# A transformer block's last output tile: its last unit multiplied in two halves of 256 columns, the final norm's weight and factor in one operation, three output transfers

## The chip, the cores and the metric

One core of a Trainium2 chip runs the whole program. The metric is the device time of one execution in microseconds: the median of three runs before the change is 460.51 us (459.75 to 461.1). The profiled execution took 460.2 us; its first and last instruction lie 458.5 us apart (the span), and 1.7 us lie around them. All times below are microseconds from the span's start unless a length is meant.

## The reference

The input is 256 tokens of width 1024 in float32. One layer: a norm, a projection, three kinds of attention (8 heads of 64 each), gates, an output projection, and then the part that matters here:

```
h   = rmsnorm(x, norm_mlp)
hid = square(relu(h @ w_up))          # [256, 4096]
x   = x + hid @ w_down                # [256, 1024]
out = rmsnorm(x, norm_final)          # x * rsqrt(mean(x*x) + 1e-6) * norm_final
```

The final norm needs the sum of squares over all 1024 columns of a token before any column of its output can be written.

## The kernel before

Every matrix product is made of three: each float32 operand is split into a high part and a remainder (`whi` and `wlo` of the weights, `u_hi` and `u_lo` of the activations), and high x high, low x high and high x low are added up in PSUM. Weights come from memory on the SP queue (`raw`, 1 MB each), ScalarE makes the high part and VectorE the remainder.

The last product is `token_major("d", 32, ...)` at line 752: 32 units of 128 rows of `w_down`. There are four output tiles of 128 tokens by 512 columns, called (t, e): t is the half of the tokens, e the half of the columns. With `by_half` the two tiles of one e stand in one PSUM tensor `ptok` of two banks, one bank each. The first 28 units are done for all four tiles in turn; the last 4 (`tail`) are done tile by tile in the order (0,0), (0,1), (1,0), (1,1), 12 matmuls of 512 columns each (4 units x 3 terms), and after each tile `ready`, here `finish`, is called, so that its work lies beside the next tile's matmuls. After (1,1) nothing is left for TensorE.

`finish` (lines 734 to 750) does this for a tile:

- VectorE adds the product, scaled by `var[t]`, to the residual `x1` (line 736; from PSUM).
- ScalarE squares and sums the first half of the tile's columns (line 232), VectorE the second half (line 233), and VectorE adds the two to what is known so far (line 241, `total`).
- For e = 0, GpSimd multiplies the tile by the norm's weight `g_fin` into `xg` (line 739).
- For e = 1, GpSimd raises `total` to the power -0.5 (line 246, `rstd`), VectorE multiplies the tile by `g_fin` meanwhile (line 743), and then ScalarE scales 384 columns of `xg` by `rstd` (line 747) and VectorE 640 (line 749); each part goes out by its own transfer (line 750), ScalarE's on the ACT queue and VectorE's on the SP queue.

Each engine runs its instructions in the order in which they stand; what another engine makes is waited for at a semaphore, and the waits are put in by the framework from the tiles that an instruction reads and writes.

Of the kernel before, what the change touches and what calls it, by code (L numbers as in the profile page):

```python
# [8 lines left out]
F32 = mybir.dt.float32  # L9
F32R = mybir.dt.float32r  # L10
AF = mybir.ActivationFunctionType
ALU = mybir.AluOpType
PSUM = bass.MemoryType.PSUM

P = 128
S = 256
NT = S // P
D = 1024
# [6 lines left out]
EPS = 1e-6  # L25
# [12 lines left out]
def hybrid_attention_block(ctx, tc, x, norm_mix, w_in, b_forget, w_branch, w_out,  # L38
# [4 lines left out]
    nc = tc.nc  # L43
# [19 lines left out]
    small = ctx.enter_context(tc.tile_pool(name="small", bufs=4))  # L63
# [8 lines left out]
    out = out[0]  # L72
# [27 lines left out]
    ready = {}  # L100
    state = {"next": 0, "used": 0}
# [27 lines left out]
    def weights(which, br, j, i):  # L129
        return ready[which, br, j, i]  # L130

    def used(n=1):

        state["used"] += n
        pump()

    def follow(later, earlier):

        tc.add_manual_dep(later.ins, earlier.ins.name, mybir.DependencyInfo(
            mybir.DependencyClass.NoSync, mybir.DependencyReason.DATA), reason="order on one engine")  # L140
# [7 lines left out]
    def terms(o, pairs, first, last, **kw):  # L148

        for i, (l, r) in enumerate(pairs):  # L150
            nc.tensor.matmul(o, l, r, start=first and i == 0, stop=last and i == len(pairs) - 1, **kw)  # L151
# [77 lines left out]
    def square_sum(src, junk, ss):  # L229

        n = src.shape[-1] // 2
        nc.scalar.activation(junk[:, 0:n], src[:, 0:n], AF.Square, accum_out=ss[:, 0:1])
        nc.vector.tensor_tensor_reduce(junk[:, n:], src[:, n:], src[:, n:], 1.0, 0.0, ALU.mult, ALU.add, ss[:, 1:2])

    def total_square(src, junk, so_far=D * EPS):


        ss = small.tile([P, 2], F32, name="ss", tag="ss")
        square_sum(src, junk, ss)
        total = small.tile([P, 1], F32, name="total", tag="total")  # L240
        made = nc.vector.scalar_tensor_tensor(total, ss[:, 0:1], so_far, ss[:, 1:2], op0=ALU.add, op1=ALU.add)
        return total, made

    def rsqrt(ms):
        rstd = small.tile([P, 1], F32, name="rstd", tag="rstd")
        nc.gpsimd.tensor_tensor(rstd, ms, minus_half, op=ALU.pow)
        return rstd
# [392 lines left out]
    def token_major(which, n_units, hi, lo, tail, order, by_half, ready):  # L640

        pair = [ps.tile([P, 2, 512], F32, name="ptok", tag="s2", bufs=2) for i in range(2)]
        tiles = {(t, e): pair[e][:, t] if by_half else pair[t][:, e] for t in range(NT) for e in range(2)}

        def part(u, t, e, which_terms=(0, 1, 2)):
            c = slice(t * P, (t + 1) * P)
            d = slice(e * 512, (e + 1) * 512)
            wh, wl = weights(which, 0, u // 2, u % 2)
            pairs = [(hi[:, u, c], wh[:, 0, d]), (lo[:, u, c], wh[:, 0, d]), (hi[:, u, c], wl[:, 0, d])]
            terms(tiles[t, e], [pairs[i] for i in which_terms], u == 0 and 0 in which_terms,  # L650
                  u == n_units - 1 and 2 in which_terms)

        for u in range(n_units - tail):
            for some in ((0, 1), (2,)):
                for t in range(NT):
                    for e in range(2):
                        part(u, t, e, some)
            used()
        for t, e in order:
            for u in range(n_units - tail, n_units):  # L660
                part(u, t, e)
            ready(t, e, tiles[t, e])
        used(tail)


    x1 = late.tile([P, NT, D], F32, name="x1")
    for t in range(NT):
        nc.sync.dma_start(x1[:, t], x[t * P:(t + 1) * P])
    g_fin = late.tile([P, D], F32, name="g_fin")
# [16 lines left out]
    def transpose_in(t, e):  # L686
# [4 lines left out]
        if t == 1:  # L691
            for i in range(2):
                split_gain(pts[i], 4 * e + 2 * i, g_mlp, h2[:, :, 0], h2[:, :, 1])

    token_major("o", 8, m_hi, m_lo, 4, [(0, 0), (1, 0), (0, 1), (1, 1)], False, mixed_in)

    mlp = ctx.enter_context(tc.tile_pool(name="mlp", bufs=1))
# [24 lines left out]
    var = []  # L722
    ys = late.tile([P, NT, D], F32, name="ys", tag="m_hi")
# [6 lines left out]
    xg = late.tile([P, D], F32, name="xg", tag="m_lo")  # L730
    sums = {}
    nc.gpsimd.tensor_scalar(g_fin, g_fin, ROOT_D, 0.0, op0=ALU.mult, op1=ALU.add)

    def finish(t, e, p_):
        d = slice(e * 512, (e + 1) * 512)
        nc.vector.scalar_tensor_tensor(x1[:, t, d], p_, var[t], x1[:, t, d], op0=ALU.mult, op1=ALU.add)
        sums[t], made = total_square(x1[:, t, d], ys[:, t, d], sums.get(t, D * EPS))
        if e == 0:
            nc.gpsimd.tensor_tensor(xg[:, d], x1[:, t, d], g_fin[:, d], op=ALU.mult)  # L739
        if e == 0:  # L740
            return
        rstd = rsqrt(sums[t])
        done = nc.vector.tensor_tensor(xg[:, d], x1[:, t, d], g_fin[:, d], op=ALU.mult)
        follow(done, made)
        for i, c in enumerate((slice(0, 384), slice(384, D))):
            if i == 0:
                nc.scalar.activation(ys[:, t, c], xg[:, c], AF.Copy, scale=rstd)  # L747
            else:
                nc.vector.tensor_scalar(ys[:, t, c], xg[:, c], rstd, None, op0=ALU.mult)
            (nc.scalar, nc.sync)[i].dma_start(out[t * P:(t + 1) * P, c], ys[:, t, c])  # L750

    token_major("d", 32, u_hi, u_lo, 4, [(0, 0), (0, 1), (1, 0), (1, 1)], True, finish)


# [26 lines left out]
```

## Time and profile before

| | us |
|---|---|
| median of three runs | 460.51 |
| profiled execution | 460.2 |
| its span | 458.5 |
| TensorE matmul busy | 446.5 (97%) |
| VectorE busy | 326.0 (71%) |
| ScalarE busy | 273.6 (60%) |
| GpSimd busy | 38.5 (8%) |

The page gives busy time, the span in 40 slices, the chain of work that ended last, and the costliest groups of instructions. For a change at the program's very end the single instructions of the last 8 us in order of time say more than the sums: which starts when, how long it takes, and what it had waited for. A row of that view gives the start, the length, the engine (PE is TensorE's matmul, PEld its weight load, DVE VectorE, ACT ScalarE, POOL GpSimd; a q behind the name is the engine's queue, which issues transfers), the line, the operation, output<-inputs, the shape, and in brackets the idle time before it and who ended it.

### The profile page before, as it was taken

The numbers are of one execution on the slowest core, as the hardware profiler recorded it, in microseconds if no ns is written. First come the engines' busy times: TensorE is split into PE (matmuls) and PEld (weight loads), VectorE is DVE, ScalarE is ACT, GpSimd is POOL, SyncE is SP. The second block draws the span as 40 slices with busy tenths as digits, with TensorE's granted clock in tenths as the row PEclk, the third lists the DMA queues.
The fourth block names the chain that finished last, engine by engine and source line by source line (L and its number), as shares of the span: only waits on it lengthen the run. The fifth ranks groups of instructions, "written<-read, shape, count | busy, mean of one in ns | idle before, by whom it ended". The sixth has DMA issues, their size and how long they took to land. (4 is left out here: it accounts for less than half of the span.)

```text
span 458.5 us, 6837 instructions
## 1 busy us (share of the span) xinstructions
PE 446.5 (97%) x2575; PEld 391.8 (85%) x2575; DVE 326.0 (71%) x543; ACT 273.6 (60%) x474; POOL 38.5 (8%) x75
## 2 busy tenths in 40 slices
PE   6999999999999999999999998999999999999993
PEld 3989998999899888888888887888888888888882
DVE  6878777888788878559759769877778864444425
ACT  5759997788567886556557446555556653334302
POOL 6503210213000000000000000000000000000012
PEclk9999999999999999999999999999999999999998
DMA  8768563445354448556556617766665576555202
GB/s 299 255 191 277 164 191 99 147 146 169 97 167 150 139 126 290 182 183 184 183 188 216 201 41 238 219 185 183 185 183 184 183 256 203 183 185 183 93 0 92
DMA packets 58002, 80.71 MB, mean 176 GB/s; under 512 B 2521, under 2 KB 45809, under 8 KB 57969
## 3 DMA queue, kind: packets, MB, share of 16 engines
q1 hardware_dynamic: 57632, 79.87, 54.1%
q8 instruction: 20, 0.33, 0.3%
q10 hardware_dynamic: 336, 0.40, 0.2%
q14 instruction: 14, 0.11, 0.1%
HBM read 79.21 MB, written 1.06 MB: 175 GB/s over the span
## 5 line engine op out<-in xcount | busy, mean ns | idle before, releaser
L125 DVE TENSOR_TENSOR wlo_d<-raw,whi_d 128x1024 fp32r<-128x1024 f32 x32 | 39.1, 1225 | 35.2 <-ACT whi_d L122 35.2
L151 PE MATMUL pu<-h,whi_u 128*128 128x512 f32 x256 | 61.4, 391 | 1.2 <-DVE h L260 1.2
L122 ACT ACTIVATE whi_d<-raw 128x1024 fp32r<-128x1024 f32 x32 | 33.8, 1059 | 42.3 <-PE ptok L151 34.2
L151 PEld LDWEIGHTS pu<-h,whi_u 128*128 128x128 f32 x256 | 46.9, 188 | 10.6 <-DVE h L260 1.5
L151 PE MATMUL ptok<-whi_d,u_lo 128*128 128x512 f32 x128 | 49.8, 389 | 0.0
L151 PE MATMUL ptok<-whi_d,u_hi 128*128 128x512 f32 x128 | 49.8, 389 | 0.0
L151 PE MATMUL pg<-hT,whi_g 128*128 128x512 f32 x192 | 46.7, 392 | 0.0
L122 ACT ACTIVATE whi_u<-raw 128x1024 fp32r<-128x1024 f32 x32 | 33.3, 1059 | 22.2 <-DMA raw<-in_w_up_dram 20.7
L125 DVE TENSOR_TENSOR wlo_u<-raw,whi_u 128x1024 fp32r<-128x1024 f32 x32 | 38.9, 1221 | 9.8 <-ACT whi_u L122 9.7
L151 PEld LDWEIGHTS pg<-hT,whi_g 128*128 128x128 f32 x192 | 35.1, 188 | 6.7
L125 DVE TENSOR_TENSOR wlo_g<-raw,whi_g 128x1024 fp32r<-128x1024 f32 x24 | 29.3, 1223 | 10.9 <-ACT whi_g L122 5.9
L151 PE MATMUL ptok<-wlo_d,u_hi 128*128 128x512 f32 x128 | 36.2, 389 | 0.0
L151 PEld LDWEIGHTS pu<-h,wlo_u 128*128 128x128 f32 x256 | 33.0, 191 | 1.3
L122 ACT ACTIVATE whi_g<-raw 128x1024 fp32r<-128x1024 f32 x24 | 25.4, 1058 | 14.3 <-PE pg L151 3.4
L151 PE MATMUL pu<-h,wlo_u 128*128 128x256 f32 x256 | 33.4, 283 | 0.0
L151 PEld LDWEIGHTS ptok<-whi_d,u_lo 128*128 128x128 f32 x128 | 24.0, 188 | 5.0
L151 PEld LDWEIGHTS ptok<-whi_d,u_hi 128*128 128x128 f32 x128 | 24.0, 188 | 5.0
L151 PEld LDWEIGHTS ptok<-wlo_d,u_hi 128*128 128x128 f32 x128 | 24.0, 188 | 5.0
L151 PEld LDWEIGHTS pg<-hT,wlo_g 128*128 128x128 f32 x192 | 25.1, 191 | 1.3
L151 PE MATMUL pg<-hT,wlo_g 128*128 128x256 f32 x192 | 25.5, 282 | 0.0
L739 POOL TENSOR_TENSOR xg<-x,g_fin 128x512 f32<-128x512 f32 x2 | 2.9, 1472 | 265.6 <-issue 264.2
L125 DVE TENSOR_TENSOR wlo_b<-raw,whi_b 128x1024 fp32r<-128x1024 f32 x12 | 14.7, 1223 | 10.5 <-PE pg L151 9.1
(498 smaller groups left out, 939.7 us busy)
## 6 DMA issues: line engine op xcount, KB each, us to landing
raw<-in_w_in_dram SPq DMA_DIRECT2D x29, 1024.0 KB, 5.0
raw<-in_w_up_dram SPq DMA_DIRECT2D x16, 1024.0 KB, 5.5
raw<-in_w_down_dram SPq DMA_DIRECT2D x16, 1024.0 KB, 4.8
raw<-in_w_branch_dram SPq DMA_DIRECT2D x6, 1024.0 KB, 5.0
raw<-in_w_out_dram SPq DMA_DIRECT2D x4, 1024.0 KB, 4.9
x_sb<-in_x_dram SPq DMA_DIRECT2D x2, 512.0 KB, 3.9
raw<-in_w_in_dram SPq DMA_DIRECT2D x2, 512.0 KB, 5.5
rows<-c_rows SPq DMA_DIRECT2D x8, 128.0 KB, 4.8
```

Source lines behind the costliest of these rows:

```text
L122: nc.scalar.activation(hi, raw, AF.Copy)
L125: (nc.gpsimd if n == 0 and i else nc.vector).tensor_tensor(lo, raw, hi.bitcast(F32), op=ALU.subtract)
L151: nc.tensor.matmul(o, l, r, start=first and i == 0, stop=last and i == len(pairs) - 1, **kw)
L739: nc.gpsimd.tensor_tensor(xg[:, d], x1[:, t, d], g_fin[:, d], op=ALU.mult)
```

## The change

For the last tile (1,1) alone, the last unit's three matmuls of 512 columns become two times three of 256 columns (`half=0`, then `half=1`; `S` is 256), and `finish` is called after each half. The first call adds the residual and has ScalarE square and sum the whole half (256 columns, line 753); the second adds the residual of the other half, adds the first half's sum to the total (`partly`, line 758), and squares its 256 columns by the pair of lines 232 and 233, 128 columns each.

For both token halves, VectorE no longer multiplies columns 512 to 1023 by `g_fin` ahead (line 743 goes). Once `rstd` is there, ScalarE scales columns 256 to 511 of `xg` and then 0 to 255 (line 769), and VectorE multiplies columns 512 to 767 and then 768 to 1023 of `x1` by `rstd` and by `g_fin` in one operation (line 773). Three transfers follow: columns 256 to 767 and then 768 to 1023 on the SP queue, 0 to 255 on the ACT queue; before, there were 0 to 383 on ACT and 384 to 1023 on SP.

```diff
@@ -642,13 +642,15 @@
         pair = [ps.tile([P, 2, 512], F32, name="ptok", tag="s2", bufs=2) for i in range(2)]
         tiles = {(t, e): pair[e][:, t] if by_half else pair[t][:, e] for t in range(NT) for e in range(2)}
 
-        def part(u, t, e, which_terms=(0, 1, 2)):
+        def part(u, t, e, which_terms=(0, 1, 2), half=None):
             c = slice(t * P, (t + 1) * P)
-            d = slice(e * 512, (e + 1) * 512)
+            n = 512 if half is None else S
+            at_ = slice((half or 0) * n, (half or 0) * n + n)
+            d = slice(e * 512 + at_.start, e * 512 + at_.stop)
             wh, wl = weights(which, 0, u // 2, u % 2)
             pairs = [(hi[:, u, c], wh[:, 0, d]), (lo[:, u, c], wh[:, 0, d]), (hi[:, u, c], wl[:, 0, d])]
-            terms(tiles[t, e], [pairs[i] for i in which_terms], u == 0 and 0 in which_terms,
-                  u == n_units - 1 and 2 in which_terms)
+            terms(tiles[t, e][:, at_], [pairs[i] for i in which_terms], u == 0 and 0 in which_terms,
+                  u == n_units - 1 and 2 in which_terms, skip_group_check=half == 1)
 
         for u in range(n_units - tail):
             for some in ((0, 1), (2,)):
@@ -657,9 +659,16 @@
                         part(u, t, e, some)
             used()
         for t, e in order:
-            for u in range(n_units - tail, n_units):
+            split = by_half and (t, e) == order[-1]
+            for u in range(n_units - tail, n_units - split):
                 part(u, t, e)
-            ready(t, e, tiles[t, e])
+            if split:
+
+                for i in range(2):
+                    part(n_units - 1, t, e, half=i)
+                    ready(t, e, tiles[t, e], i)
+            else:
+                ready(t, e, tiles[t, e])
         used(tail)
 
 
@@ -731,23 +740,39 @@
     sums = {}
     nc.gpsimd.tensor_scalar(g_fin, g_fin, ROOT_D, 0.0, op0=ALU.mult, op1=ALU.add)
 
-    def finish(t, e, p_):
+    def residual(t, d, p_):
+        nc.vector.scalar_tensor_tensor(x1[:, t, d], p_, var[t], x1[:, t, d], op0=ALU.mult, op1=ALU.add)
+
+    def finish(t, e, p_, half=None):
         d = slice(e * 512, (e + 1) * 512)
-        nc.vector.scalar_tensor_tensor(x1[:, t, d], p_, var[t], x1[:, t, d], op0=ALU.mult, op1=ALU.add)
-        sums[t], made = total_square(x1[:, t, d], ys[:, t, d], sums.get(t, D * EPS))
+        c = slice(d.start + S * (half or 0), d.start + S * (half + 1) if half is not None else d.stop)
+        residual(t, c, p_[:, c.start - d.start:c.stop - d.start])
+        if half == 0:
+
+            ss = small.tile([P, 1], F32, name="ss1", tag="ss1", bufs=1)
+            nc.scalar.activation(ys[:, t, c], x1[:, t, c], AF.Square, accum_out=ss)
+            state["ss"] = ss
+            return
+        if half == 1:
+            partly = small.tile([P, 1], F32, name="partly", tag="partly", bufs=1)
+            nc.vector.tensor_tensor(partly, sums[t], state["ss"], op=ALU.add)
+            sums[t] = partly
+        sums[t], made = total_square(x1[:, t, c], ys[:, t, c], sums.get(t, D * EPS))
         if e == 0:
             nc.gpsimd.tensor_tensor(xg[:, d], x1[:, t, d], g_fin[:, d], op=ALU.mult)
-        if e == 0:
             return
         rstd = rsqrt(sums[t])
-        done = nc.vector.tensor_tensor(xg[:, d], x1[:, t, d], g_fin[:, d], op=ALU.mult)
-        follow(done, made)
-        for i, c in enumerate((slice(0, 384), slice(384, D))):
-            if i == 0:
-                nc.scalar.activation(ys[:, t, c], xg[:, c], AF.Copy, scale=rstd)
-            else:
-                nc.vector.tensor_scalar(ys[:, t, c], xg[:, c], rstd, None, op0=ALU.mult)
-            (nc.scalar, nc.sync)[i].dma_start(out[t * P:(t + 1) * P, c], ys[:, t, c])
+
+        inner = slice(S, 3 * S)
+        for i in range(2):
+            c = slice((1 - i) * S, (2 - i) * S)
+            nc.scalar.activation(ys[:, t, c], xg[:, c], AF.Copy, scale=rstd)
+            if i:
+                nc.scalar.dma_start(out[t * P:(t + 1) * P, c], ys[:, t, c])
+            c = slice(512 + i * S, 512 + (i + 1) * S)
+            nc.vector.scalar_tensor_tensor(ys[:, t, c], x1[:, t, c], rstd, g_fin[:, c], op0=ALU.mult, op1=ALU.mult)
+            c = c if i else inner
+            nc.sync.dma_start(out[t * P:(t + 1) * P, c], ys[:, t, c])
 
     token_major("d", 32, u_hi, u_lo, 4, [(0, 0), (0, 1), (1, 0), (1, 1)], True, finish)
 
```

The two new columns `ss1` and `partly` lie in the pool `small`. The pools allotted behind it on that side, `mid` (attention outputs, gates) and `mlp` (`u_hi`, `u_lo`), move by 64 bytes a partition; no other tile moves.

The order of instructions changes at the end of the program alone. On TensorE, the last rows of tile (1,1), before and now (`whi_d_4436` and `wlo_d_4437` are the last unit's weights; what stands in brackets is the engine whose semaphore the instruction waits for):

```order
 L151 MATMUL ptok<-wlo_d_4421,u_hi 128x512
-L151 MATMUL ptok<-whi_d_4436,u_hi 128x512
-L151 MATMUL ptok<-whi_d_4436,u_lo 128x512
-L151 MATMUL ptok<-wlo_d_4437,u_hi 128x512
-L776 UNCONDITIONAL_BRANCH
+L151 MATMUL ptok<-whi_d_4436,u_hi 128x256
+L151 MATMUL ptok<-whi_d_4436,u_lo 128x256
+L151 MATMUL ptok<-wlo_d_4437,u_hi 128x256
+L151 MATMUL ptok<-whi_d_4436,u_hi 128x256 [waits DVE_49]
```

The first matmul of the second half has a wait on VectorE (in the program the semaphore value is the one that the first half's residual, line 744, raises); two more matmuls of 256 columns follow it.

On VectorE, from the residual of tile (1,1) to the end of the program, before (`x_2970` is `x1`; the ISA rows are line 233's square sum and the read of its accumulator):

```order
L736 SCALAR_TENSOR_TENSOR x_2970<-ptok,v__4004,x_2970 128x512 [waits PE_49]
L233 ISA ys,ss<-x_2970 128x256 [waits DVE_49]
L233 ISA ss 128x1
L241 SCALAR_TENSOR_TENSOR total<-ss,total 128x1 [waits DVE_49,Activation_49]
L743 TENSOR_TENSOR xg<-x_2970,g_fin 128x512
L749 TENSOR_SCALAR ys<-xg,rstd 128x640 [waits DVE_49,Pool_49]
```

And the same stretch now (`ss_4554` is `ss1`, which ScalarE makes):

```order
L744 SCALAR_TENSOR_TENSOR x_2970<-ptok,v__4004,x_2970 128x256 [waits PE_49] x2
L758 TENSOR_TENSOR partly<-total,ss_4554 128x1 [waits Activation_49]
L233 ISA ys,ss<-x_2970 128x128 [waits DVE_49]
L233 ISA ss 128x1
L241 SCALAR_TENSOR_TENSOR total<-ss,partly 128x1 [waits DVE_49,Activation_49]
L773 SCALAR_TENSOR_TENSOR ys<-x_2970,rstd,g_fin 128x256 [waits Pool_49]
L773 SCALAR_TENSOR_TENSOR ys<-x_2970,rstd,g_fin 128x256
```

The residual and the square are in smaller pieces, `partly` is new between them, and the multiplication by `g_fin` has gone from ahead of the wait for GpSimd to behind it.

## Rows read from the trace of the kernel before

**Rows 1.** The chain that ended last, a piece near its end: start, length, what.

```profile
451.58 1.61 issue
```

**Rows 2.** Timeline of TensorE, the last unit of tile (1,1).

```profile
450.72 0.39 PE L151 MATMUL ptok<-whi_d,u_hi 128*128 128x512 f32 x1
...
451.17 0.39 PE L151 MATMUL ptok<-wlo_d,u_hi 128*128 128x512 f32 x1
```

**Rows 3.** Timeline of VectorE at the end.

```profile
449.23 0.74 DVE L736 SCALAR_TENSOR_TENSOR x<-ptok,v__4004,x 128x512 f32<-128x512 f32 x1
...
450.55 1.04 DVE L241 SCALAR_TENSOR_TENSOR total<-ss 128x1 f32<-128x1 f32 x1
451.60 0.75 DVE L736 SCALAR_TENSOR_TENSOR x<-ptok,v__4004,x 128x512 f32<-128x512 f32 x1
...
452.93 0.22 DVE L241 SCALAR_TENSOR_TENSOR total<-ss,total 128x1 f32<-128x1 f32 x1
453.06 0.68 DVE L743 TENSOR_TENSOR xg<-x,g_fin 128x512 f32<-128x512 f32 x1
454.20 0.55 DVE L749 TENSOR_SCALAR ys<-xg,rstd 128x640 f32<-128x640 f32 x1 [0.46 <-POOL rstd L246]
```

**Rows 4.** Timeline of GpSimd, at the start and at the end.

```profile
5.39 0.56 POOL L246 TENSOR_TENSOR rstd<-total,minus_half 128x1 f32<-128x1 f32 x1 [1.80 <-DVE total L241]
...
447.79 0.93 POOL L246 TENSOR_TENSOR rstd<-total,minus_half 128x1 f32<-128x1 f32 x1 [1.99 <-DVE total L241]
450.11 1.47 POOL L739 TENSOR_TENSOR xg<-x,g_fin 128x512 f32<-128x512 f32 x1 [1.38 <-ACT ys L747]
453.23 0.94 POOL L246 TENSOR_TENSOR rstd<-total,minus_half 128x1 f32<-128x1 f32 x1 [1.65 <-DVE total L241]
```

**Rows 5.** Timeline of ScalarE and of the queues at the end.

```profile
452.38 0.42 ACT L232 ACTIVATE ys<-x 128x256 f32<-128x256 f32 x1 [1.87 <-DVE x L736]
...
454.20 0.61 ACT L747 ACTIVATE ys<-xg,rstd 128x384 f32<-128x384 f32 x1 [1.31 <-POOL rstd L246]
...
454.83 0.36 SPq L750 DMA_DIRECT2D out_dram<-ys  x1
454.85 0.38 ACTq L750 DMA_DIRECT2D out_dram<-ys  x1
```

**Rows 6.** One line's instructions, L750: from the ACT queue's issue to landing.

```profile
DMA to landing us min/median/max: 2.7/2.7/2.7
```

**Rows 7.** Stretches of 0.25 us: busy, PEclk, share of DMA engines, GB/s.

```profile
455.50:455.75 0.25, 0.00 (x0) 0.00 (x0) 0.00 (x0) 0.00 (x0) 0.00 (x0) 0.50 0.23 92
455.75:456.00 0.25, 0.00 (x0) 0.00 (x0) 0.00 (x0) 0.00 (x0) 0.00 (x0) 0.50 1.02 410
...
457.00:457.25 0.25, 0.00 (x0) 0.00 (x0) 0.00 (x0) 0.00 (x0) 0.00 (x0) 0.50 0.09 25
```

**Rows 8.** Timeline: VectorE's and TensorE's first rows after a wait, and a 256-column run.

```profile
277.41 1.66 DVE L260 SCALAR_TENSOR_TENSOR h<-ptr,g_col,h 128x256 fp32r<-128x256 f32 x4
...
277.95 0.96 PE L151 MATMUL pu<-h,whi_u 128*128 128x512 f32 x3 [1.23 <-DVE h L260]
...
301.19 2.08 PE L151 MATMUL pu<-h,wlo_u 128*128 128x256 f32 x16
```

**Rows 9.** Instructions of tiles h, pu and ys by line: min/median/max ns.

```profile
L260 DVE SCALAR_TENSOR_TENSOR h<-ptr,g_col,h x8: 473/473/483, 271.0 to 278.6; 128x256 fp32r<-128x256 f32 x8
L151 PE MATMUL pu<-h,wlo_u x256: 277/283/283, 275.2 to 364.2; 128*128 128x256 f32 x128
L232 ACT ACTIVATE ys<-x x6: 416/418/645, 274.4 to 452.4; 128x256 f32<-128x256 f32 x4, 128x512 f32<-128x512 f32 x2
```

**Rows 10.** Groups by line: VectorE's two-factor form with all inputs in SBUF.

```profile
L717 DVE SCALAR_TENSOR_TENSOR r<-r 128x512 f32<-128x512 f32 x16 | 11.1, 692 | 0.5
```

**Rows 11.** Two transfers of 512 KB issued together on SP: the issue, and to landing.

```profile
0.80 0.86 SPq L182 DMA_DIRECT2D x_sb<-in_x_dram  x2
...
DMA to landing us min/median/max: 3.5/3.9/4.3
```

## The prediction

> **What bounds the kernel now.** I read the page first: TensorE's matmuls are busy for 446.5 of 458.5 us, and the change touches nothing before the last unit of the last tile, so only the stretch from 450.7 to the end can change. I went on to the chain that ended last. It is of little use here: from 451.58 it says "issue" for 1.61 us [rows 1], where the timelines show work on three engines. So I read the single instructions in order of time, engine by engine.
>
> The last matmul starts at 451.17 and ends at 451.56 [rows 2]. VectorE adds the residual from 451.60 for 0.75 [rows 3]; the squares start at 452.38 on ScalarE [rows 5]; the total starts at 452.93 on VectorE [rows 3]; GpSimd raises it to the power from 453.23 for 0.94, so `rstd` is there at 454.17 [rows 4]. Both scalings start at 454.20 and take 0.61 and 0.55; the transfers are issued at 454.83 and 454.85 [rows 3, 5]. Data move at 410 GB/s from about 455.69 (92 GB/s in a quarter of a microsecond is 0.06 us at that rate, before 455.75) to about 457.02 (25 GB/s likewise is 0.02 us, after 457.00) [rows 7]: 1.33 us for 512 KB. The ACT queue's transfer lands 2.7 after its issue, at 457.55 [rows 5, 6], and the span ends 0.95 later. No part of this stretch is TensorE; it is one chain of dependent steps.
>
> Two things in it are easily missed. First, the power takes 0.56 us when VectorE runs nothing beside it (at 5.39) and 0.93 or 0.94 at the end [rows 4], where VectorE's product `xg` (line 743) starts 0.17 before it and runs to 453.74 [rows 3]; GpSimd is done 0.43 after that. The two hold each other up. Second, VectorE's `total` of tile (1,0), an operation on one column, takes 1.04 us instead of 0.22 and ends at 451.59, when GpSimd's product ends (450.11 and 1.47 make 451.58) [rows 3, 4]. So VectorE comes free for the last residual only just in time, and not by chance: GpSimd holds it.
>
> **The change part by part.**
>
> *The split of the last unit.* 16 matmuls of 256 columns span 2.08 us; less the last one's 0.283 and over 15 steps that is 0.120 a step [rows 8, 9]. So the first half starts at 450.72 as now, its third matmul at 450.96, and it ends at 451.24; its residual could start at 451.28, at the 0.04 that lies between 451.56 and 451.60 now. But VectorE is held by the one-column total until GpSimd's product of tile (1,0) ends. When is that? For the first 128 tokens the power also loses its company: 0.56 for 0.93, so `rstd` comes at 448.35 instead of 448.72. Against this, two fused operations stand in front of tile (1,0)'s residual where one of 0.55 stood. A 256-column operation with a pointer factor takes 0.473 [rows 9], and the next one on VectorE starts about 0.08 before the end of the last (452.93 and 0.22 against 453.06) [rows 3]: 448.39, 448.78, and the residual at 449.17 instead of 449.23. GpSimd's product follows the residual as now (it also waits for ScalarE's second scaling, which reads the same `xg` and ends by 449.4, before the residual does), so it ends at 451.52 instead of 451.58, and the first half's residual starts at 451.54: the half that was ready 0.32 early gains 0.06.
>
> It takes 0.47, to 452.01. The second half's first matmul waits for exactly this residual, as the order of instructions shows, though the two touch different columns. Behind it on TensorE stand only the two other matmuls, and all that is left of the program waits for them. TensorE's start after a wait on VectorE can be seen once: the first of four operations from 277.41 ends at 277.88, and the matmul starts at 277.95, 0.07 later; three matmuls then span 0.96 where steps of 0.227 and a length of 0.39 would give 0.84 [rows 2, 8, 9]. I take 0.07 and 0.11. So: matmuls from 452.08; 0.11 and two steps of 0.12 and 0.283 make 452.71; residual from 452.75 to 453.22. It ends at 452.35 now. The split costs 0.87.
>
> The Trainium skill has a rule that speaks against this split: "PSUM — Partial Sum Buffer", section "PSUM bank collisions raise a hardware error", says that engines have to be kept apart by bank and quarter of the partitions, not by address, so two halves of one bank can't be written and read at the same time. No run here shows a collision; the wait in the order is what that rule asks for. By the rule the sum stands as worked out; if columns could be kept apart, the second half would end at 451.60, its residual at about 452.4, and `rstd` would come some 0.8 earlier.
>
> *Squares and total.* They start 0.03 after the residual, at 453.25. ScalarE's square of 512 columns takes 0.645 and of 256 0.418 [rows 9], so 128 columns fewer save 0.11; the total starts 0.55 after the squares now (452.38 to 452.93), then 0.44: 453.69. The first half's square on ScalarE (0.42, from 452.04) is over before the second residual starts, and `partly`, one column, lies before VectorE's square, which is shorter than ScalarE's pair; I cost both at nothing. If `partly` isn't hidden it costs the 0.22 of a total [rows 3].
>
> *The power.* It starts 0.30 after the total, at 453.99. Line 743 is gone and VectorE has only waiting instructions, so I take the 0.56 of the undisturbed row: 454.55. The other end is the 0.94 of now.
>
> *Weight and factor in one operation.* From 454.59: VectorE's first 256 columns to 455.06 and the second from 454.98 to 455.45. The bounds are 0.42 (512 columns with all inputs in SBUF take 0.692, less 256 at the 0.27 by which 0.75 exceeds 0.473) and 0.473 [rows 3, 9, 10]; I take the one that has the pointer factor too. ScalarE's first 256 columns take 0.61 less 0.11, to 455.09. Before, 640 columns took 0.55.
>
> A second rule of the Trainium skill speaks against this part: "VectorE: DVE Perf Modes", section "The perf-mode tier table (the rule you actually need)", has `tensor_scalar` at twice the rate of `tensor_tensor` for float32 in SBUF. The rows agree (640 columns in 0.55, 512 of the two-input form in 0.69), so the fused form gives up the faster rate behind `rstd`: VectorE's last piece is ready 0.90 behind it instead of 0.58. Left as it was, the part would be ready 0.3 sooner; whether the end moves by that depends on the transfers.
>
> *Three transfers.* The first SP issue is 0.08 behind the later of its two writers, at 455.17 (454.83 now); its 0.36 of issue ends at 455.53, when the second piece is ready too; ACT issues at about 455.5. Data start 0.86 after the first issue, at 456.03. 256 KB take 0.65, so until 456.70 the stream is busy, and the other two transfers' data are due from 456.4: no gap. Two transfers of 512 KB issued together on SP land 3.5 and 4.3 after issue [rows 11], so the queue does not wait for one landing before it starts the next. 512 KB in all take 1.33 as now: 457.36, landing 457.89, end 458.84.
>
> **Sum.** The split +0.87, squares -0.11, power -0.38: `rstd` at 454.55 instead of 454.17, and the end 0.34 later, since the first issue comes 0.04 sooner after `rstd`. The profiled 460.2 becomes 460.5. The profiled run lies 0.3 below the median, so for the median I add 0.34 to 460.51: 460.85, or 460.9.
>
> Low end: no hold by GpSimd (-0.26), a free restart (-0.18), fused operations at 0.42 (-0.1): 460.3. High end: `partly` not hidden and no gain in the squares (+0.33), power still 0.94 (+0.38), a restart twice as dear (+0.18): 461.7.
>
> **Rivals.**
>
> *The power's gain wins* (460.3, faster by 0.2). GpSimd's product ends early enough not to hold the first residual, and TensorE restarts at once. For it: `rstd` of the first tokens is 0.37 earlier. Against: the fused operations take 0.31 of it back before GpSimd can start. Chance 0.2.
>
> *SP's second transfer waits for the first to land* (461.9). It would start its data 0.86 after 457.2 and need 0.33, 0.53 and 0.95 more: 459.9, 1.4 later than now. It decides once its data start after 457.0. For it: nothing at the end shows two transfers on SP. Against: the pair above landed 1.2 apart. Chance 0.06.
>
> *The moved tiles* (459 or 463). `u_hi` and `u_lo` lie 64 bytes on, and 384 matmuls of the last product load from them. A step of 0.227 changed by 4 ns is 1.5 us. For it: no row shows a tile at two such places. Against: 256 matmuls whose operands lie at that many places of their tiles take 277 to 283 ns each [rows 9]. Chance 0.1, half of it each way and half of it too small to see.
>
> *The forecast* (460.9): chance 0.64; its own range is 460.3 to 461.7.
>
> A measurement of this kernel can tell about 0.3%, 1.4 us, from no change: the three runs lie 1.35 apart. The forecast and the first rival lie within it; slower takes the serial transfers and part of the moved tiles and of the high end, 0.09; faster is the moved tiles' other half and what medians may scatter, 0.06. With half the runs' spread on either side the range is 459.6 to 462.1.
>
> **What would show it.** Right: a gap on TensorE of about 0.8 us between the third and the fourth 256-column matmul; VectorE's one-column total of tile (1,0) still about 1.0 long; the power 0.56; SP's second issue right behind the first; data without a gap. Wrong: the fourth matmul right behind the third; a power of 0.9; a gap in the transfers; or any change of the step of 0.227 before 450.

## The result, and the profile after

The changed kernel takes 463.61 us (median of six runs, 462.73 to 465.31), the kernel before in the same series 460.67 (459.75 to 461.54): a ratio of 1.0065, interval 1.0047 to 1.0083 (ratios and intervals are estimated from all the runs, so they need not be the quotient of the two medians). The prediction was 460.9, no change; the kernel is slower by 2.9 us. The profiled execution took 462.87 us with a span of 461.1, against 460.2 and 458.5: 2.6 us more between its first and last instruction.

Where do the 2.6 us lie? I cut the span at two rows that both traces have: the first matmul of the last product, and the first matmul of the last unit of tile (1,1). Here and below the span's end is read to 0.01 us (458.49 before, 461.13 after).

| us | before | after | difference |
|---|---|---|---|
| span's start to the first matmul of the last product | 364.33 | 364.17 | -0.16 |
| from there to the last unit of tile (1,1), 381 matmuls | 86.39 | 88.90 | +2.51 |
| from there to the span's end | 7.77 | 8.06 | +0.29 |

The last product's first row before, and after (the last unit's first rows are in [rows 2] and further down):

```profile
364.33 0.40 PE L151 MATMUL ptok<-whi_d,u_hi 128*128 128x512 f32 x1
```

```profile
364.17 0.40 PE L151 MATMUL ptok<-whi_d,u_hi 128*128 128x512 f32 x1
```

The end, of which the whole prediction speaks, got 0.29 us longer; its sum was +0.34. The loss is in the 381 matmuls ahead of it, which the change leaves alone. The view by stretches shows it for 40 us in the middle of them. Its columns are: start and end, length, TensorE's matmul busy time and number, then the same for weight load, VectorE, ScalarE and GpSimd, the granted clock, the share of the DMA engines and GB/s. The kernel before:

```profile
400.00:440.00 40.00, 40.00 (x178) 33.14 (x177) 15.94 (x13) 12.80 (x13) 0.00 (x0) 1.00 0.39 133
```

The kernel after:

```profile
400.00:440.00 40.00, 40.00 (x173) 32.21 (x172) 15.94 (x13) 13.64 (x13) 0.00 (x0) 1.00 0.41 141
```

TensorE is busy without a pause in both and the granted clock is 1.00 (the higher of its two levels, 2.4 GHz) in both, but 173 matmuls fit where 178 did. The engine's waits can't show this, and its busy share only rises. The step from one start to the next tells it: 86.39 us over 381 steps is 226.7 ns, 88.90 is 233.3 ns. Before, the starts follow each other at 226 or 227 ns all along from the sixth on; after, at 231 and 236 in turn from the second on. The view of tile `u_hi` gives minimum, median and maximum of each form in ns; before:

```profile
L151 PEld LDWEIGHTS ptok<-whi_d,u_hi x128: 187/188/192, 364.2 to 450.5; 128*128 128x128 f32 x128
L151 PE MATMUL ptok<-whi_d,u_hi x128: 389/389/396, 364.3 to 450.7; 128*128 128x512 f32 x128
```

and after:

```profile
L151 PEld LDWEIGHTS ptok<-whi_d,u_hi x129: 186/188/192, 364.1 to 454.2; 128*128 128x128 f32 x129
L151 PE MATMUL ptok<-whi_d,u_hi x129: 281/393/398, 364.2 to 454.2; 128*128 128x512 f32 x127, 128*128 128x256 f32 x2
```

The weight load, which reads `u_hi`, is as long as before (188); the median of the matmul rows rises from 389 to 393.

The end itself answers to [rows 2 to 5]. TensorE, from the last matmul of 512 columns:

```profile
452.84 0.39 PE L151 MATMUL ptok<-wlo_d,u_hi 128*128 128x512 f32 x1
453.07 0.28 PE L151 MATMUL ptok<-whi_d,u_hi 128*128 128x256 f32 x1
453.19 0.28 PE L151 MATMUL ptok<-whi_d,u_lo 128*128 128x256 f32 x1
453.31 0.28 PE L151 MATMUL ptok<-wlo_d,u_hi 128*128 128x256 f32 x1
454.21 0.38 PE L151 MATMUL ptok<-whi_d,u_hi 128*128 128x256 f32 x1 [0.62 <-DVE x L744]
```

VectorE:

```profile
452.72 1.04 DVE L241 SCALAR_TENSOR_TENSOR total<-ss 128x1 f32<-128x1 f32 x1
453.68 0.47 DVE L744 SCALAR_TENSOR_TENSOR x<-ptok,v__4004,x 128x256 f32<-128x256 f32 x1
454.87 0.48 DVE L744 SCALAR_TENSOR_TENSOR x<-ptok,v__4004,x 128x256 f32<-128x256 f32 x1 [0.72 <-PE ptok L151]
455.27 0.15 DVE L758 TENSOR_TENSOR partly<-total,ss 128x1 f32<-128x1 f32 x1
455.39 0.29 DVE L233 CUSTOM_DVE_ANT_0 ys<-x 128x128 f32<-128x128 f32 x1
...
455.82 0.22 DVE L241 SCALAR_TENSOR_TENSOR total<-ss,partly 128x1 f32<-128x1 f32 x1
456.72 0.88 DVE L773 SCALAR_TENSOR_TENSOR ys<-x,rstd,g_fin 128x256 f32<-128x256 f32 x2 [0.67 <-POOL rstd L246]
```

GpSimd:

```profile
452.37 1.38 POOL L762 TENSOR_TENSOR xg<-x,g_fin 128x512 f32<-128x512 f32 x1 [1.81 <-DVE x L744]
456.12 0.56 POOL L246 TENSOR_TENSOR rstd<-total,minus_half 128x1 f32<-128x1 f32 x1 [2.38 <-DVE total L241]
```

TensorE waits 0.62 for the first half's residual, VectorE's one-column total is still held for 1.04 until GpSimd's product ends (453.75), and the power takes 0.56. SP issues its two transfers from 457.28, 0.60 after `rstd`. The stretches of the output's transfers, with the same columns as above, answer to [rows 7]:

```profile
458.00:458.25 0.25, 0.00 (x0) 0.00 (x0) 0.00 (x0) 0.00 (x0) 0.00 (x0) 0.50 0.49 197
458.25:458.50 0.25, 0.00 (x0) 0.00 (x0) 0.00 (x0) 0.00 (x0) 0.00 (x0) 0.50 1.08 385
458.50:458.75 0.25, 0.00 (x0) 0.00 (x0) 0.00 (x0) 0.00 (x0) 0.00 (x0) 0.50 0.99 385
458.75:459.00 0.25, 0.00 (x0) 0.00 (x0) 0.00 (x0) 0.00 (x0) 0.00 (x0) 0.50 1.06 373
459.00:459.25 0.25, 0.00 (x0) 0.00 (x0) 0.00 (x0) 0.00 (x0) 0.00 (x0) 0.50 1.06 373
459.25:459.50 0.25, 0.00 (x0) 0.00 (x0) 0.00 (x0) 0.00 (x0) 0.00 (x0) 0.50 1.04 357
459.50:459.75 0.25, 0.00 (x0) 0.00 (x0) 0.00 (x0) 0.00 (x0) 0.00 (x0) 0.50 0.10 29
```

There is no gap between the three transfers: no stretch between the first and the last falls below 357 GB/s.

### The profile page after: what moved, and what is told of

Read it like the earlier page. It is cut to its first block, busy times and chain, and to the rows that moved or that the text cites. A ratio compares the mean times of both kernels' runs of the same rounds, so it can differ in the third digit from the quotient of the medians.

```text
span 461.1 us, 6849 instructions
## 1 busy us (share of the span) xinstructions
PE 450.2 (98%) x2578; PEld 392.1 (85%) x2578; DVE 326.0 (71%) x545; ACT 274.9 (60%) x478; POOL 37.6 (8%) x75
## 4 chain that ended last, share of the span: by engine, by line
PE 95%; DVE 1%; DMA 1%; issue 1%; POOL 1%; ACT 0%; POOLq 0%; SPq 0%; DVEq 0%
PE ptok L151 23%; PE pu L151 19%; PE pg L151 14%; PE pqk L151 14%; PE pv L151 7%; PE pqk L346 1%; DMA x_sb<-in_x_dram 1%; PE po L145 1%; PE po L144 1%; PE po L146 1%; PE ptr L252 1%; PE pf L151 0%; PE z L424 0%; PE pT L463 0%; PE pT L462 0%
## 5 line engine op out<-in xcount | busy, mean ns | idle before, releaser
L151 PE MATMUL ptok<-whi_d,u_lo 128*128 128x512 f32 x129 | 51.1, 396 | 0.0
L151 PE MATMUL ptok<-wlo_d,u_hi 128*128 128x512 f32 x129 | 37.2, 394 | 0.0
```

## The experiments

My theory after the result: the 64 bytes by which `u_hi` and `u_lo` moved make every matmul that is loaded from them 6.6 ns longer, and the edits at the end cost what the prediction's sum says. In the built program `u_hi` starts at byte 109056 of each partition before, a multiple of 512, and at 109120 after; `u_lo` lies 32768 further in both. The rival: the edits themselves, or something that the longer program brings, slow the stage. `filler(pool, n)` in the diffs allots n bytes that nothing uses, so it moves what is allotted behind. Where no number of runs is given, the time is that of one execution. Two executions of one kernel lie up to 4.5 us apart, so such a time decides nothing here; the lengths in its trace do.

**The change with the tiles in their old places.**

```diff
@@ the kernel after
-    filler(small, 128)
+    filler(small, 64)
```

> The whole change, but the filler of pool small is 64 bytes shorter, so that u_hi and u_lo (and the tiles of mid) lie where they lay before the change. Theory A (the place of u_hi and u_lo sets the step of the last product): the step goes back from 0.2335 to 0.227 us, and only the tail's cost is left: 0.2 to 0.4 us above the kernel before, about 460.9. Theory B (the longer step comes from something else in the change, such as the order of the program's end, its length, or the alignment of the engines in time): the step stays 0.2335 and the time about 463.6.

Measured: 460.71 us (12 runs) against 460.49 (20 runs), ratio 0.9997, interval 0.9981 to 1.0013. The last product is back at 86.39 us, to the hundredth, and 178 matmuls fit into the 40 us again:

```profile
400.00:440.00 40.00, 40.00 (x178) 33.13 (x177) 15.93 (x13) 13.10 (x13) 0.00 (x0) 1.00 0.40 136
```

From the last unit to the span's end it takes 8.18 (451.02 to 459.20), 0.41 more than before. So the edits alone are the "no change" of the prediction, and the 2.5 us belong to the place.

**The kernel before with its tiles moved by 64 bytes.**

```diff
@@ the kernel before
-    filler(small, 128)
+    filler(small, 192)
```

> The kernel before with nothing changed but 64 bytes more of filler in pool small, which moves mid and mlp (u_hi, u_lo) as the change does. Theory A: the step of the last product goes from 0.227 to 0.2335 us and the time up by 384 x 0.0066 = 2.5 us, to about 463.1. Theory B: step 0.227, no difference, 460.7.

Measured: 463.04 us (7 runs) against 460.49, ratio 1.0058, interval 1.0037 to 1.0080; the last product takes 88.90 us, steps of 231 and 236:

```profile
400.00:440.00 40.00, 40.00 (x173) 32.25 (x172) 15.93 (x13) 13.81 (x13) 0.00 (x0) 1.00 0.42 145
```

Not one instruction differs from the kernel before but in its addresses: the rival falls.

**The two tiles alone, without the pool `mid`.** The pool `mid` moves with `mlp` in all of this, and in some runs the small columns of `small` do; here only `mlp` moves.

```diff
@@ the kernel before, in the pool mlp, ahead of u_hi
+    filler(mlp, 64, "ahead")
```

> Kernel before with 64 bytes put ahead of u_hi in its own pool, so that u_hi and u_lo (the operands that TensorE loads as 128x128 in the last product) lie 64 bytes further, and the tiles of the pool mid stay where they were. If the place of these two tiles decides: step of the last product's 512-column matmuls 231/236 ns, about 463 us. If the tiles of mid decide: step 226/227 ns, 460.5 us.

Measured: 462.83 us, the last product 88.90 us:

```profile
400.00:440.00 40.00, 40.00 (x173) 32.24 (x172) 15.93 (x13) 13.81 (x13) 0.00 (x0) 1.00 0.41 144
```

173 matmuls again. It is the move of `u_hi` and `u_lo`.

**One of the two.**

```diff
@@ the kernel before, in the pool mlp, between u_hi and u_lo
+    filler(mlp, 64, "between")
```

> The kernel before with 64 bytes of filler between u_hi and u_lo, so that u_lo alone lies 64 bytes further on. Theory A in the form that each weight load's own address counts: only steps into a load of u_lo (one in three) grow, by 4 to 9 ns: 128 x 0.004 to 0.009 = 0.5 to 1.2 us. Theory A in the form that the distance of the load from the moving operand counts: the same third. Theory A in the form that the whole pipeline falls into a slower beat: all steps grow, about 2.5 us. Theory B: nothing changes.

Measured: 462.63 us. The last product takes 87.37 us, 0.98 more than before, where a third of the loads come from the moved tile: 39% of the 2.51. (In this execution the product also started at 365.77 instead of 364.33; between executions of all these kernels that start varies from 363.9 to 366.9, which is why I compare from it and not from the span's start.) The matmul rows of `u_lo`, minimum, median and maximum:

```profile
L151 PE MATMUL ptok<-whi_d,u_lo x128: 389/397/400, 366.0 to 453.4; 128*128 128x512 f32 x128
```

and those of the low weights with the unmoved `u_hi`:

```profile
L151 PE MATMUL ptok<-wlo_d,u_hi x128: 389/389/397, 367.6 to 453.6; 128*128 128x512 f32 x128
```

The third kind, the high weights with `u_hi`, stands next to the first in the order and has a median of 392. The cost goes with the operand that lies off and reaches its neighbours. The expectation that only the steps into a load of `u_lo` grow is not borne out: from the ninth step on, the step to a matmul with `u_lo` takes 228.8 ns in the mean, the step from it 232.9 where the high weights follow and 230.1 where the low ones do, and the others 226.9 and 227.4.

**Which places are good?** Three more shifts of the kernel before: by 128, 512 and 256 bytes.

```diff
@@ the kernel before; 256, then 640, then 384
-    filler(small, 128)
+    filler(small, 256)
```

> The kernel before with 128 bytes more of filler in pool small. Theory A with a period of 128 bytes (u_hi starts at a multiple of 128 again, as before): step 0.227, no difference. Theory A with a longer period (a multiple of 512 is needed, which u_hi had before): step longer, by 4 to 9 ns. Theory B: nothing changes.

> The kernel before with 512 bytes more of filler in pool small, so that u_hi and u_lo start at a multiple of 512 bytes again (109568). If a multiple of 512 is what the fast step needs: 0.227 us, no difference to the kernel before. If the distance to the weights' tiles counts in a longer period (these lie 512 behind a multiple of 1024, as u_hi did before): 0.230 us or more, some 1 to 2.5 us slower.

> Kernel before with u_hi and u_lo 256 bytes further (u_hi at 109312, a multiple of 256 and not of 512). If a multiple of 256 is enough: step 226/227 ns, about 460.5 to 461.5 us. If it takes a multiple of 512: a mean step above 228 ns and a last product longer by (step - 226.7) x 384.

Measured: by 128 bytes 463.18 us, the product 88.53 (232.4 ns a step); by 512 bytes 461.33, 86.39; by 256 bytes 461.27, 86.39. The row by 256 bytes:

```profile
400.00:440.00 40.00, 40.00 (x178) 33.10 (x177) 15.94 (x13) 13.79 (x13) 0.00 (x0) 1.00 0.42 144
```

and by 128 bytes:

```profile
400.00:440.00 40.00, 40.00 (x174) 32.43 (x173) 16.12 (x14) 13.79 (x13) 0.00 (x0) 1.00 0.41 149
```

So the old addresses are nothing special, and 512 is more than is needed: a start at a multiple of 256 bytes gives the short step, 64 and 128 beyond one don't.

**The change, with its tiles moved on to a multiple of 512.** This repairs the change in the other direction, at addresses that no earlier kernel of the two had.

```diff
@@ the kernel after
-    filler(small, 128)
+    filler(small, 576)
```

> The whole change, with u_hi moved on by 448 bytes more, to 109568, the next multiple of 512, so that every tile of the two pools lies at an address that neither kernel had. If the multiple of 512 decides: step 226/227 ns in the last product and the time of the change in the old places, 460.7 us, ratio 1.000. If the old addresses as such are special: 231/236 ns and 463 us.

Measured: 461.60 us (10 runs) against 461.51 (13 runs), ratio 1.0016, interval 0.9995 to 1.0036; the product 86.39 us, from the last unit to the end 8.17. As expected, though the interval is wide: starts of the last product scatter in these runs too (366.89 in the profiled one).

The remaining four runs weigh the terms of the sum at the end, all with the tiles in their old places; lengths are from the start of the last unit to the span's end, 7.77 before.

**The split alone**, with the ending of the kernel before (line 743's product, two transfers).

```diff
@@ the kernel after, old places
-            nc.vector.scalar_tensor_tensor(ys[:, t, c], x1[:, t, c], rstd, g_fin[:, c], op0=ALU.mult, op1=ALU.mult)
...
+        done = nc.vector.tensor_tensor(xg[:, d], x1[:, t, d], g_fin[:, d], op=ALU.mult)
+        follow(done, made)
...
```

> The split of the last unit alone, with the ending of the kernel before (line 743's product, two transfers) and the tiles where they lay. If the split costs what it did beside the other parts: TensorE stands still for 0.75 us between the halves, the power takes 0.94 again since VectorE's product lies beside it, and the end lies 8.5 us behind the last unit's first matmul. Rival (the split itself is free, and the ending costs): 7.8 us.

Measured: 460.5 us; 8.50 (450.26 to 458.76), so +0.73, where the prediction's +0.87 and -0.11 make 0.76. TensorE's wait and the power, which has line 743 (here 765) beside it again:

```profile
451.59 0.39 PE L151 MATMUL ptok<-whi_d,u_hi 128*128 128x256 f32 x1 [0.81 <-DVE x L744]
...
453.34 0.68 DVE L765 TENSOR_TENSOR xg<-x,g_fin 128x512 f32<-128x512 f32 x1
453.50 0.94 POOL L246 TENSOR_TENSOR rstd<-total,minus_half 128x1 f32<-128x1 f32 x1 [2.38 <-DVE total L241]
```

**The whole change, with the second half in another PSUM bank.** Its first 31 units of these 256 columns are left out, so only its times at the end mean something.

```diff
@@ the kernel after, old places
+                other = ps.tile([P, 512], F32, name="other", tag="dense", bufs=3)
...
-                    part(n_units - 1, t, e, half=i)
-                    ready(t, e, tiles[t, e], i)
+                    o = (None, other)[i]
+                    part(n_units - 1, t, e, half=i, o=o)
+                    ready(t, e, other if i else tiles[t, e], i)
```

> The whole change with the old places, but the second half's three matmuls go into another PSUM bank, and the second residual reads that bank: the first 31 units of these 256 columns are left out of the output, the instructions and their sizes stay. If the wait is for the shared PSUM tensor: TensorE goes on with the second half 0.12 us after the third matmul, both residuals follow one another on VectorE, and the end lies 7.4 us behind the last unit's first matmul (8.18 with the wait). Rival (VectorE, held by GpSimd's product, is the bound in any case): 7.8 us or more.

Measured: 460.04 us; 7.42 (450.91 to 458.33), 0.76 less than the 8.18 with one bank:

```profile
451.14 0.28 PE L151 MATMUL ptok<-wlo_d,u_hi 128*128 128x256 f32 x1
451.26 0.28 PE L151 MATMUL other<-whi_d,u_hi 128*128 128x256 f32 x1
451.38 0.28 PE L151 MATMUL other<-whi_d,u_lo 128*128 128x256 f32 x1
451.50 0.28 PE L151 MATMUL other<-wlo_d,u_hi 128*128 128x256 f32 x1
```

The fourth matmul now stands right behind the third, and the two residuals follow each other at 451.65 and 452.05. The wait is worth as much as the split costs (0.73); without it the change would end 0.35 sooner than the kernel before. `other` is another tensor as well as another bank, so this run does not tell by which of the two the wait goes. The Trainium skill, "PSUM — Partial Sum Buffer", section "PSUM bank collisions raise a hardware error", asks for engines to be kept apart by bank rather than by address; the wait of 0.75 between two halves of one bank that share no column agrees with that rule.

**The other edits without the split.**

```diff
@@ the kernel after
-            split = by_half and (t, e) == order[-1]
+            split = False
```

> The change without the split of the last unit and with the tiles where they lay before it (no new columns in pool small): the fused operation and the three transfers alone. If the power's gain is real and the split's wait is what eats it: the power takes 0.56 us, rstd lies 0.38 sooner behind the last matmul than in the kernel before, and the span from the last unit's first matmul to the end is 7.4 us (7.78 before, 8.18 with the split); the time 0.3 us below the kernel before. Rival (the fused form and the third transfer give the gain back behind rstd): 7.7 to 7.9 us. By the time alone the two can hardly be told apart.

Measured: 462.12 us (12 runs) against 461.04 (17 runs), ratio 1.0026, interval 1.0006 to 1.0046: the expected gain isn't there. At the end the profiled execution needs 6.98 from the last residual to the span's end, 6.89 before. The power is 0.56 as expected, but the total ahead of it comes late. Is that a matter of one execution? I ran it again.

> A second execution of the change without the halves in the old places, for its tail alone: from the last residual's start to the end 6.94 us were measured, with the total of the last tokens formed 0.89 us after the squares began. If that was a matter of one execution: 0.55 us, and 6.5 to 6.6 us to the end. If it is in the program: 6.9 us again.

Measured: 461.0 us, 6.98 from the residual (452.31) to the end (the 6.94 of the expectation goes by a span rounded to 0.1), and the same late total:

```profile
453.10 0.42 ACT L232 ACTIVATE ys<-x 128x256 f32<-128x256 f32 x1 [1.92 <-DVE x L744]
...
453.42 0.19 ACT L232 ACTIVATION_READ_ACCUMULATOR ys<-x 128x1 f32 x1
...
453.99 0.22 DVE L241 SCALAR_TENSOR_TENSOR total<-ss,total 128x1 f32<-128x1 f32 x1 [0.46 <-ACT ys L232]
454.29 0.56 POOL L246 TENSOR_TENSOR rstd<-total,minus_half 128x1 f32<-128x1 f32 x1 [2.04 <-DVE total L241]
```

ScalarE's sum is there at 453.61, and VectorE starts 0.38 later. In the kernel before that is 0.04: its total starts at 452.93 [rows 3], and the sum's row is

```profile
452.71 0.18 ACT L232 ACTIVATION_READ_ACCUMULATOR ys<-x 128x1 f32 x1
```

What VectorE does in between no row shows, and it stays open. It is of this variant: in the whole change the total starts 0.43 after the squares, as predicted. So what the shorter power gains here (0.56 for 0.94) is used up: 0.34 goes to the late total (0.89 after the squares instead of 0.55), and 0.12 is lost behind `rstd`, from where both executions need 4.44 to the span's end and the kernel before 4.32. Why this variant's median lies 1.1 us above is open too, since its last product takes 86.39 and its end is within 0.1 of before. In both kept executions the excess lies ahead of the last product, which starts at 365.69 and 365.05 (364.33 before); that start scatters between executions of every kernel here, and two don't tell whether this variant has a part in it.

## Why the prediction was wrong

**What failed** is its first step, "the change touches nothing before the last unit of the last tile, so only the stretch from 450.7 to the end can change". The change allots two columns, and with them it moves the operands of 384 matmuls. The prediction had this as a rival, *the moved tiles* at 459 or 463, and left it at 0.1. Its arithmetic was right in form; the size taken for an example, 4 ns, is 6.6, and 381 x 6.6 ns is 2.5 us.

**Why it was priced so low** can be seen in its argument against: "256 matmuls whose operands lie at that many places of their tiles take 277 to 283 ns each" [rows 9]. These places lie 128 float32 numbers, 512 bytes, apart. Seen from a multiple of 256 they are all the same place. The row holds fixed the one thing that it was meant to vary, so it was no evidence at all. With no other row for either side, an effect of some us deserved far more than a part of one tenth (and the parts named, half each way and half too small to see, make more than the whole). That the address before is a multiple of 512 and after it is not stood in the built program and was to be had without a run.

**The terms of the sum**, against the changed kernel (with the tiles off) and the one with its tiles in their old places:

| us | predicted | after | old places |
|---|---|---|---|
| last unit to first half's residual | 0.82 | 0.61 | 0.74 |
| third to fourth matmul of 256 columns | 1.12 | 0.90 | 1.03 |
| fourth matmul to second residual | 0.67 | 0.66 | 0.66 |
| second residual to squares | 0.50 | 0.52 | 0.52 |
| squares to total | 0.44 | 0.43 | 0.43 |
| the power | 0.56 | 0.56 | 0.56 |
| `rstd` to the span's end | 4.29 | 4.45 | 4.45 |
| all, against before | +0.34 | +0.29 | +0.41 |

The first two rows overlap, and the 0.30 from the total to the power, alike in all three, has no row, so a column is not a sum. That +0.34 comes so close is luck in part: in the old places the wait came 0.09 shorter and the end 0.16 longer than worked out.

- *The split*: right, in mechanism and size (+0.73 measured alone, with the squares, where 0.76 was worked out). GpSimd's product of tile (1,0) holds the first residual as worked out; the residual starts 0.08 (old places) to 0.21 (changed kernel) sooner after the last unit's start.
- *Squares, `partly`*: right. `partly` lies under ScalarE's wait at no cost.
- *The power*: right. 0.56 with line 743 gone, 0.94 with it back, in the split alone.
- *Weight and factor in one operation*: two of 256 columns take 0.88 together, as worked out (455.45 - 454.59 is 0.86).
- *Transfers*: no gap, but the end comes 4.45 after `rstd`, 0.16 later than predicted. With the old ending it is 4.32, in the kernel before and in the split alone; so the new ending costs 0.13 where the prediction had a gain of 0.04. Data move at 357 to 385 GB/s instead of 410, from about 458.12 to 459.52, which is 1.40 for 1.33, and from there the span's end is 1.61 away, before 1.47 (from 457.02). How much of it is the operation on weight and factor and how much the third transfer, no run separates. (In the working, 456.03 and 0.65 make 456.68, not 456.70; nothing hangs on it.)
- *The range*: its upper end is not what its own rule gives. 461.7 and half of the runs' 1.35 make 462.4, not 462.1; the measured 463.6 lies beyond both.

**The rivals.** *The power's gain wins* falls: the end is longer in every kernel that has the split in one bank. (By the low end's terms, 0.26 and 0.18, its two conditions would have made 460.4, not 460.3.) *SP's second transfer waits* falls: no gap in the transfers. *The moved tiles* is what happened, on its slow side. The sign that the prediction named, "any change of the step of 0.227 before 450", is what the trace shows.

**Open.** Why a weight operand 64 or 128 bytes past a multiple of 256 lengthens the step: the load's row stays at 188 ns, so the trace shows the effect on the matmuls and not its way. Whether the place itself counts or its distance from the weights that stream against the loaded operand: in the built programs of all runs the weight tiles `whi_d` and `wlo_d` start 512 bytes past a multiple of 1024, so each shift changed both at once. Other distances than 64, 128, 256 and 512 were not tried, nor other stages. No version here is faster than the kernel before beyond what can be measured.

## What to carry to other kernels

An edit that allots a tile moves every tile behind it: compare the addresses of the large matmul operands before and after, modulo 256 bytes here, before weighing the instructions, and pad the pool so that they keep their place. A row speaks for or against a cause only if the cause varies in it. When an engine is busy all the time before and after, compare its steps (matmuls in a fixed stretch), since neither waits nor busy shares show that each became 3% longer.

## What was not expected of the hardware

The step of back-to-back matmuls of 512 columns, each with its own load of 128x128 float32 weights, depends on where in SBUF the loaded operand starts (or on its distance from the streamed weights, which were never moved): 226.7 ns at 109056, 109312 and 109568 (multiples of 256), 233.3 at 109120 and 232.4 at 109184, at a granted clock of 1.00 in all. It is repeatable: the 381 steps took 86.39 us in eight kernels with the operand on a multiple of 256 and 88.90 in all three with it 64 bytes past one. The Trainium skill, "SBUF — State Buffer", section "Operand start alignment", asks only for a multiple of the element size and says that this is about legality and not about speed; these runs show that there is a price in time as well, 2.5 us of 460.
